# A two-layer decoder trunk: matmul operands moved to multiples of 128 bytes in SBUF, with a padded stride between the K blocks of the activations

## The chip, the cores and the metric

The kernel runs on one core of one Trainium2 chip, as one launch. The metric is the device time of that launch in microseconds (us); a figure for a kernel is the median of several runs. The engines are named as in the profile: PE is TensorE's matrix multiplication, PEld its loading of weights (the stationary operand), DVE is VectorE, ACT is ScalarE, POOL is GpSimd and SP is SyncE, which issues most DMAs.

## What is computed

The reference is a trunk of two decoder layers on one sequence of 256 tokens with 1024 features. Each layer has a feed-forward network (FFN), a token mixer and a second FFN. Ahead of each stands an RMS norm whose output is shifted and scaled by values that come from a conditioning vector `c`; behind each, a gate from `c` scales what is added to the stream.

```python
for layer in range(DEPTH):                       # DEPTH = 2
    if layer == N_A_LAYERS:                      # keys, values and forget gates, once
        k_sh, v_sh, F_sh = shared_kv(x, c_act, ...)
    mod = c_act @ ada_w[layer] + ada_b[layer]    # shifts, scales and gates
    h = modulate(rms_norm(x, norm_g[layer, 0]), sh1, sc1)
    x = x + 0.5 * g1 * swiglu(h, ffn_w_in[layer, 0], ffn_w_out[layer, 0])
    h = modulate(rms_norm(x, norm_g[layer, 1]), sh2, sc2)
    mix = diff_attention(h, ...) if layer < N_A_LAYERS else forgetting_attention(h, ...)
    x = x + g2 * mix
    h = modulate(rms_norm(x, norm_g[layer, 2]), sh3, sc3)
    x = x + 0.5 * g3 * swiglu(h, ffn_w_in[layer, 1], ffn_w_out[layer, 1])
return rms_norm(x, final_g)
```

`swiglu` is `(silu(h @ w_gate) * (h @ w_up)) @ w_out` with 2816 hidden features. All data are float32.

## The kernel before

**Layout.** Features lie on the 128 partitions, tokens along the free axis. The stream `x`, the normed input and the hidden features are therefore arrays of blocks of 128 features by 256 tokens. The normed input, 8 such K blocks, is held as two tiles, `HH` and `HL` (lines 391 and 392); the hidden features as 11 pairs of tiles `hidh0` to `hidh10` and `hidl0` to `hidl10` (lines 526 and 527), each with two K blocks of 256 columns.

**Three products for one.** A float32 number is split into a high part of type float32r and the rest, also float32r. A product then is three matmuls into the same PSUM bank (`mm3`, line 383): high weight by high input, low weight by high input, high weight by low input. `HH`, `hidh` and `wh` are high parts; `HL`, `hidl` and `wl` low ones. Nearly every matmul has a 128x128 weight block as its stationary operand, and 256 columns of the input as the moving one; each has its own weight load, which runs while the matmul ahead of it streams. Where the input is taken ahead of its norm (tiles lp, lg, lu), two extra columns beside each K block of `HH` and `HL` carry the shift: a row of a K block has `SX` = 258 floats. In the V projection (`v_proj`, line 698) the roles are exchanged: blocks of `HH` and `HL` are stationary and 512 columns of weights stream.

**The FFN** (`ffn`, line 518). In the first phase a group of 256 gate and 256 up features is made at a time: two banks, `pg` and `pu`, and for each of the 8 K blocks four weight blocks of 128 columns, three matmuls each, 12 matmuls a K block and 96 a group. There are 38 such groups in the four FFNs (7, 10, 11 and 10); the other features of the first FFN are made in eight banks (`pf`), those of the two "late" FFNs in `lg` and `lu`. In the second phase each of 8 output blocks `po` sums 22 K blocks of hidden features, 66 matmuls; K blocks 2j and 2j+1 come from `hidh{j}` and `hidl{j}`. The hidden tiles are used again by the attention layers under other names.

**The weights** come from DRAM in parts of up to 1024 columns into one of six `raw` tiles, are copied to one of six `wh` tiles by ScalarE, and VectorE writes the rest into one of five `wl` tiles (lines 262 to 294).

**Order.** Each engine keeps the order in which the program issues its instructions. `InOrder` (line 56) wraps each engine and runs a rough clock while the program is written out: before an instruction that would have to wait, it puts background work, which is weight splits on ScalarE and VectorE and modulation columns on VectorE. That clock knows when a tile is ready by its name, and for tiles whose names begin with HH, HL or x_ by the offset too (line 83).

**Modulation.** Every shift, scale and gate is a column tile of 8 floats a partition, `mod_...`, with a derived one `modx_...` for scales and some gates (lines 195 and 204). `ada_block` fills one column with a multiply and sum on VectorE.

**The norm.** `rstd_of` (line 433) makes 1/rms: ScalarE writes a first estimate `r0`, VectorE refines it in three steps and writes the last into a tile `rstd` of its own.

**Where tiles lie.** The tiles of a pool are laid one after the other in the order in which the program first asks for them, each rounded up to 32 bytes a partition. A tile's start therefore depends on the small tiles ahead of it: `eps`, `half`, `one`, the modulation columns, `ls`, `nlam`, `subg`, `fb` and `Fq`.

Of the kernel before, what the change touches and what calls it, by code (L numbers as in the profile page):

```python
# [10 lines left out]
F32 = mybir.dt.float32  # L11
F32R = mybir.dt.float32r
BF16 = mybir.dt.bfloat16
AF = mybir.ActivationFunctionType
ALU = mybir.AluOpType
PSUM = bass.MemoryType.PSUM

P = 128
D = 1024
S = 256  # L20
NC = D // P
HD = 64
AH = 8
BH = 16
# [7 lines left out]
K0 = 4  # L32
SX = S + 2
CP_SLACK = 0.3
SUB_SLACK = 0.2
# [20 lines left out]
class InOrder:  # L56
    """An engine whose instructions keep the order of this program.

    A rough clock of each engine (us) tells when background work fits."""

# [10 lines left out]
    def plainly(self, f):  # L71
        """f() without background work before its instructions."""
        busy, self.busy = self.busy, True
        f()
        self.busy = busy

    def __getattr__(self, name):
        f = getattr(self.engine, name)

        def call(*args, **kw):  # L80
            aps = [v for v in (*args, *kw.values()) if hasattr(v, "tensor")]
            if aps:
                names = [(v.tensor.name, v.offset if v.tensor.name[:2] in ("HH", "HL", "x_") else 0) for v in aps]
                cost = self.fixed + self.rate * math.prod(aps[0].shape[1:])
# [21 lines left out]
def trunk(ctx, tc, a, out):  # L106
# [26 lines left out]

# [1 line left out]
    crow = ap_.tile([P, 2, D], F32, tag="ada", name="crow").rearrange("p a b -> p (a b)")  # L135
# [15 lines left out]
    dve.memset(one, 1.0)  # L151
    cact = cp_.tile([P, D], F32, name="cact")

    def table(func):
        act.preload_act_table(func)

# [1 line left out]
    mods = {}  # L158
# [27 lines left out]
    def ada_block():  # L186
        """One column block of one modulation; a load follows each second one."""
        u, i = divmod(ada_done[0], 2)
# [5 lines left out]
        if m not in mods:  # L194
            mods[m] = [cp_.tile([P, NC], F32, name=f"mod_{m[0]}_{m[1]}"), None]
        mt = mods[m][0]
# [5 lines left out]
        if kind != 0 and m[1] != 5:  # L202
            if mods[m][1] is None:
                mods[m][1] = cp_.tile([P, NC], F32, name=f"modx_{m[0]}_{m[1]}")
            mx = mods[m][1]
            js = (j, j + 1) if m == (0, 1) else ((j - 3, j + 1) if j % 4 == 3 else None)
            if js is not None:
                js = slice(*js)
                if kind == 1:
                    gc = V_KVN if m[0] == "kv" else V_NORM + (m[0] * 3 + m[1] // 3) * NC  # L210
                    dve.scalar_tensor_tensor(
                        mx[:, js], mt[:, js], 1.0, vecs[:, gc + js.start:gc + js.stop],
                        op0=ALU.add, op1=ALU.mult)
                else:
                    dve.tensor_scalar_mul(mx[:, js], mt[:, js], 0.5)
# [7 lines left out]

# [1 line left out]
    stream = []  # L225
# [36 lines left out]
    def w_dma(count=NRAW):  # L262
        """Load the next parts of the stream, as far as the parts in their place are split."""
        while count and len(raws) < min(len(pieces), len(los) + NRAW):
# [8 lines left out]
    def cp_part():  # L273
        """Copy the next part of the stream: its high float32r half."""
        u = len(his)
# [7 lines left out]
    def sub_part():  # L283
        """The low half of the oldest copied part; its place takes the next load."""
        u = len(los)
# [13 lines left out]
    def ahead():  # L299
        """Parts copied beyond the unit in use."""  # L300
        return len(his) - begun[0]

    def take(src, split=False):
        """The next unit of the stream, split; blk(c, w) gives its columns."""
        u = taken[0]
# [20 lines left out]
    def work(cols):  # L326
        """After the products of this many columns of the stream."""
        credit[0] = min(CREDIT, credit[0] + pace[0] * 2 * cols / 2048)
        if mode[0] != "hold":
            bg()  # L330
# [6 lines left out]
    def fill_dve(start):  # L337
        """Background work before an instruction that has to wait until start."""
        while mode[0] != "hold" and dve.t + DVE_FIT < start:
# [11 lines left out]
    def bg():  # L351
        """Background work as far as it fits: splits first, then modulations at their pace."""
        while (len(his) < min(len(pieces), len(raws), done[0] + NHI)
# [35 lines left out]

# [1 line left out]
    HH = cp_.tile([P, NC, SX], F32R, name="HH")  # L391
    HL = cp_.tile([P, NC, SX], F32R, name="HL")
    hx = [(HH[:, k], HL[:, k]) for k in range(NC)]
    hn = [(HH[:, k, :S], HL[:, k, :S]) for k in range(NC)]
# [3 lines left out]
    def shift_cols(nxt):  # L398
        """The shift as an extra pair of columns beside the input."""
        shb = mods[nxt[1]][0].rearrange("p (k o) -> p k o", o=1).to_broadcast([P, NC, 2])  # L400
        act.copy(HH[:, :, S:], shb)
        dve.tensor_tensor(HL[:, :, S:], shb, HH[:, :, S:].bitcast(F32), op=ALU.subtract)

    def x_update(n, ps, gate, nxt, acc_eng):
        """x[n] += gate * ps; then g*(1+scale)*x[n] for the next product, and the square of x[n].

        Returns the second half, for VectorE after ScalarE's part."""
        dve.scalar_tensor_tensor(x[n], ps, gate[:, n:n + 1], x[n], op0=ALU.mult, op1=ALU.add)
# [24 lines left out]
    def rstd_of(then=None, parts=None):  # L433
# [10 lines left out]
        dve.scalar_tensor_tensor(ra, ra, -0.5, r0, op0=ALU.mult, op1=ALU.mult)  # L444
        r = kp.tile([P, S], F32, tag="rstd", name="rstd", bufs=1)
        dve.scalar_tensor_tensor(r, ra, 1.5, r0, op0=ALU.add, op1=ALU.mult)
        return r

    def make_h(k, r, m):
        """h[k]; returns VectorE's second half."""  # L450
        A, sh = mods[m[0]][1], mods[m[1]][0]
# [7 lines left out]
    class MakeH:  # L459
        """h chunk by chunk, VectorE's second half of each behind the first half of the next."""  # L460

# [22 lines left out]
    def late_pairs(src, dsts, m, then):  # L484
        """Two pairs of blocks of W against the input before its norm; the outputs go to dsts, normalised.

        Returns 1/rms."""
        pb = []
# [27 lines left out]

# [1 line left out]
    def ffn(l, i, kind, m, nxt, at=2):  # L518
        """kind: 1/rms for the first FFN; "late" if hx is not normalised; "ready" if it is."""
        hid = []  # L520
# [140 lines left out]
    class OutProj:  # L661
        """Residual product whose K blocks come one at a time, the last two together."""

# [7 lines left out]
        def steps(self):  # L671
            """The next K block, in eight steps."""
            k = self.k
# [24 lines left out]
    def v_proj(src, dst):  # L698
        """dst[t][nh]: [P tokens, 512 features]; a step is one K block of one half."""
        for nh in range(2):  # L700
# [18 lines left out]
    def pair_proj(src, dst, name):  # L719
        """Two 128-feature blocks of h @ W, transposed, in eight steps."""  # L720
        pq = mmbank(name)
# [13 lines left out]

# [1 line left out]
    ada_dma(2)  # L737
# [25 lines left out]

# [1 line left out]
    UW = 383  # L765
    late = {}

    def constants():
# [5 lines left out]
        sp.dma_start(raw[:, o:a["misc"].shape[1]], a["misc"][:, o:])  # L774
        # relative position bias (times 8, with the mask), skewed through DRAM
        hot, umask, relb = raw[:NB, o:o + UW], raw[:AH, o + UW:o + 2 * UW], raw[:NB, o + 2 * UW:o + 2 * UW + AH]
        o += 2 * UW + AH

        def bias():
# [9 lines left out]
            late["skew"] = skew  # L789
            # -lambda on every partition  # L790
            ls = cp_.tile([P, 2], F32, name="ls")
            lj = kp.tile([P, HD], F32, tag="w512a", name="lj")
            for i in range(2):
# [3 lines left out]
            act.activation(ls, ls, AF.Exp)  # L797
            nlam = cp_.tile([P, 1], F32, name="nlam")
            dve.scalar_tensor_tensor(nlam, ls[:, 1:2], -LAMBDA_INIT, ls[:, 0:1],
                                     op0=ALU.add, op1=ALU.subtract)  # L800
            subg = cp_.tile([P, 1], F32, name="subg")
            dve.tensor_scalar_mul(subg, vecs[:, V_SUB:V_SUB + 1], 1.0 - LAMBDA_INIT)
# [4 lines left out]

    # ================= layer A =================
    pace[0] = PACE[0]
# [165 lines left out]

    # ================= shared keys, values and forget gates =================
    kT = [cp_.tile([P, 512], F32, name=f"kT{j}") for j in range(4)]
# [32 lines left out]
    for i, (kk, n) in enumerate(v_proj("wkv", vb)):  # L1010
# [9 lines left out]
        if i == 3:  # L1020
# [3 lines left out]
            mm(pF[:, BH:2 * BH], ub[:, :P], lft[:, BH:], start=False, stop=True)  # L1024
            Fq = cp_.tile([P, 2 * BH], F32, name="Fq")
            act.copy(Fq, pF[:, :2 * BH])
# [13 lines left out]

    # ================= layer B =================
    pace[0] = PACE[4]
# [251 lines left out]
```

## Time and profile before

| | |
|---|---|
| time, median of 3 runs | 1038.09 us (1037.96 to 1039.49) |
| span of the profiled execution (first to last instruction) | 1035.3 us |
| median less that span | 2.8 us |
| mean granted TensorE clock | 0.997 |
| DMA | 265.06 MB, mean 256 GB/s |
| VectorE: weight splits `wl`, 368 instructions | 402.5 us |
| ScalarE: weight casts `wh`, 368 instructions | 349.1 us |
| VectorE: modulation columns, 160 instructions | 203.6 us |

For the profiled execution the span is the only time that is given; the runs' times are those of other executions of the same program. A row of a group in the profile has the line, the engine, the operation, output and inputs by the program's names, shape and count, then busy time and the mean duration of one in ns. Since all engine calls go through one helper, every row shows line 101, and a group is known by its tiles. The duration of a matmul runs from its start to its modelled end, and matmuls overlap; how fast they follow each other is read from their starts in the timeline (start, duration, engine, operation). In the table of stretches a row has the stretch, its length, and for PE, PEld, DVE, ACT and POOL the busy time with the number of instructions, then the granted clock, the DMA engines' busy share and GB/s.

### The profile page before, as it was taken

To read this page: it belongs to the slowest core of one execution; us is meant where nothing else is said; L and a number is where in the kernel's file an instruction comes from. 1 tells how busy PE (TensorE), PEld (TensorE's weight loads), DVE (VectorE), ACT (ScalarE), POOL (GpSimd) and SP (SyncE) were. 2 spreads that over 40 slices of the span, in tenths; PEclk is the share of its full clock that TensorE was granted. 3 is DMA by queue.
4 is the path that set the end of the run, shared out by engine and by line. 5 is a ranking of instruction groups with operands and counts; after the bars stand their busy time and mean duration, and the time that the engine had idled before them with its cause. 6 is when DMAs were issued, how large, how long until landed. Compare 5 with 4: busy or idle time off the path is not lost.

```text
span 1035.3 us, 20394 instructions
## 1 busy us (share of the span) xinstructions
PE 1013.1 (98%) x8076; PEld 975.6 (94%) x8076; DVE 820.8 (79%) x1379; ACT 563.2 (54%) x922; POOL 38.2 (4%) x64
## 2 busy tenths in 40 slices
PE   5999999999999999999999999999999999999996
PEld 4999999998999999999998999999987799999996
DVE  6978869889889998778798888879887697555553
ACT  4465545576777644445566444444575585444542
POOL 0000100000111000000000000000011010000000
PEclk9999999999999999999999999999999999999998
DMA  9988999969666798778867999888744337554561
GB/s 350 413 301 273 308 351 340 337 202 343 196 211 219 250 400 304 271 266 303 301 226 265 345 315 334 317 282 320 263 147 121 116 126 229 185 183 147 164 173 41
DMA packets 68130, 265.06 MB, mean 256 GB/s; under 512 B 7962, under 2 KB 8114, under 8 KB 57923
## 3 DMA queue, kind: packets, MB, share of 16 engines
q1 hardware_dynamic: 65810, 258.31, 71.6%
q0 software_dynamic: 1792, 4.81, 1.7%
q8 instruction: 63, 1.03, 0.4%
q10 hardware_dynamic: 432, 0.64, 0.2%
q14 instruction: 33, 0.26, 0.1%
HBM read 262.66 MB, written 2.65 MB: 256 GB/s over the span
## 4 chain that ended last, share of the span: by engine, by line
PE 93%; ACT 2%; DVE 2%; issue 1%; DMA 1%; POOL 1%; SPq 0%; DVEq 0%; ACTq 0%; POOLq 0%
PE po L101 24%; PE pg L101 21%; PE pu L101 21%; PE pf L101 5%; PE pv L101 4%; PE pw L101 3%; PE lp L101 3%; PE pqk L101 2%; PE pob L101 1%; PE lg L101 1%; PE lu L101 1%; PE pk L101 1%; PE sb L101 1%; ACT nl L101 1%; PE pq L101 1%
## 5 line engine op out<-in xcount | busy, mean ns | idle before, releaser
L101 DVE TENSOR_TENSOR wl<-raw,wh 128x1024 fp32r<-128x1024 f32 (+1 forms) x368 | 402.5, 1106 | 114.7 <-issue 29.9
L101 ACT CAST wh<-raw 128x1024 fp32r<-128x1024 f32 (+1 forms) x368 | 349.1, 956 | 239.7 <-PE pu L101 117.3
L101 DVE CUSTOM_DVE_ANT_0 ada<-ada,cact,vecs 128x1024 f32<-128x1024 f32 x160 | 203.6, 1280 | 0.0
L101 PE MATMUL po<-hidh,wh 128*128 128x256 f32 x704 | 198.0, 281 | 0.0
L101 PE MATMUL po<-hidl,wh 128*128 128x256 f32 x704 | 197.8, 281 | 0.0
L101 PE MATMUL po<-hidh,wl 128*128 128x256 f32 x704 | 197.7, 281 | 0.0
L101 PE MATMUL pg<-HH,wl 128*128 128x256 f32 x608 | 172.0, 283 | 0.0
L101 PE MATMUL pg<-HL,wh 128*128 128x256 f32 x608 | 172.0, 283 | 0.0
L101 PE MATMUL pu<-HL,wh 128*128 128x256 f32 x608 | 171.7, 282 | 0.0
L101 PE MATMUL pu<-HH,wl 128*128 128x256 f32 x608 | 171.5, 282 | 0.0
L101 PE MATMUL pg<-HH,wh 128*128 128x256 f32 x608 | 170.9, 281 | 0.0
L101 PE MATMUL pu<-HH,wh 128*128 128x256 f32 x608 | 170.8, 281 | 0.0
L101 PEld LDWEIGHTS po<-hidh,wh 128*128 128x128 f32 x704 | 132.8, 189 | 0.0
L101 PEld LDWEIGHTS po<-hidh,wl 128*128 128x128 f32 x704 | 132.5, 188 | 0.0
L101 PEld LDWEIGHTS po<-hidl,wh 128*128 128x128 f32 x704 | 132.5, 188 | 0.0
L101 PEld LDWEIGHTS pg<-HH,wh 128*128 128x128 f32 x608 | 115.2, 189 | 0.7 <-issue 0.6
L101 PEld LDWEIGHTS pu<-HH,wh 128*128 128x128 f32 x608 | 115.3, 190 | 0.0
L101 PEld LDWEIGHTS pg<-HL,wh 128*128 128x128 f32 x608 | 115.0, 189 | 0.0
L101 PEld LDWEIGHTS pu<-HL,wh 128*128 128x128 f32 x608 | 114.8, 189 | 0.0
L101 PEld LDWEIGHTS pu<-HH,wl 128*128 128x128 f32 x608 | 114.6, 188 | 0.0
L101 PEld LDWEIGHTS pg<-HH,wl 128*128 128x128 f32 x608 | 114.3, 188 | 0.0
L101 ACT CAST hidh<-hf 128x512 fp32r<-128x512 f32 x44 | 27.3, 621 | 35.6 <-DVE hf L101 35.6
(213 smaller groups left out, 1610.4 us busy)
## 6 DMA issues: line engine op xcount, KB each, us to landing
raw<-in_win SPq DMA_DIRECT2D x176, 512.0 KB, 6.0
ada<-in_ada SPq DMA_DIRECT2D x79, 1024.0 KB, 7.3
raw<-in_wout SPq DMA_DIRECT2D x64, 384.0 KB, 4.9
raw<-in_wout SPq DMA_DIRECT2D x64, 320.0 KB, 4.2
raw<-in_wqk SPq DMA_DIRECT2D x16, 512.0 KB, 5.5
raw<-in_wo SPq DMA_DIRECT2D x16, 512.0 KB, 4.6
raw<-in_wv SPq DMA_DIRECT2D x8, 512.0 KB, 6.0
raw<-in_wkk SPq DMA_DIRECT2D x8, 512.0 KB, 6.6
```

The costliest lines, as they stand in the source:

```text
L101: return self.tc.keep_in_program_order(f(*args, **kw))
```

## The change

`HH` and `HL` get rows of 288 floats in place of 258, so that a K block begins every 1152 bytes, 9 x 128; the two shift columns still stand at 256 and 257. The small tiles that lay between the large ones are collected in `small` (24 floats) and `modall` (33 x 8 floats), whose sizes, with those of the small tiles ahead of them, add up to a multiple of 128 bytes, and `Fq` is widened to 56 floats for the same purpose. `HH`, `HL`, the hidden tiles and what shares their places, `tri`, `kT`, `vb`, `raw`, `wh`, `wl` and the `qk` tiles then begin at multiples of 128 bytes; `ones` doesn't. The tile `rstd` goes: the last refinement is written over `r0`, which makes room for the padding. The planner keeps apart slices of tiles whose names begin with "mo" by their offset. All shapes and numbers that are computed stay as they were. Comments and docstrings are blank lines.

```diff
+SP_ = 288
...
-                names = [(v.tensor.name, v.offset if v.tensor.name[:2] in ("HH", "HL", "x_") else 0) for v in aps]
+                names = [(v.tensor.name, v.offset if v.tensor.name[:2] in ("HH", "HL", "x_", "mo") else 0) for v in aps]
...
     cact = cp_.tile([P, D], F32, name="cact")
+    small = cp_.tile([P, 24], F32, name="small")
+    nmods = [0]
+    modall = cp_.tile([P, 33, NC], F32, name="modall")
+
+    def mod_col():
+        nmods[0] += 1
+        return modall[:, nmods[0] - 1]
...
-            mods[m] = [cp_.tile([P, NC], F32, name=f"mod_{m[0]}_{m[1]}"), None]
+            mods[m] = [mod_col(), None]
...
-                mods[m][1] = cp_.tile([P, NC], F32, name=f"modx_{m[0]}_{m[1]}")
+                mods[m][1] = mod_col()
...
-    HH = cp_.tile([P, NC, SX], F32R, name="HH")
-    HL = cp_.tile([P, NC, SX], F32R, name="HL")
-    hx = [(HH[:, k], HL[:, k]) for k in range(NC)]
+    HH = cp_.tile([P, NC, SP_], F32R, name="HH")
+    HL = cp_.tile([P, NC, SP_], F32R, name="HL")
+    hx = [(HH[:, k, :SX], HL[:, k, :SX]) for k in range(NC)]
...
-        act.copy(HH[:, :, S:], shb)
-        dve.tensor_tensor(HL[:, :, S:], shb, HH[:, :, S:].bitcast(F32), op=ALU.subtract)
+        act.copy(HH[:, :, S:SX], shb)
+        dve.tensor_tensor(HL[:, :, S:SX], shb, HH[:, :, S:SX].bitcast(F32), op=ALU.subtract)
...
-        r = kp.tile([P, S], F32, tag="rstd", name="rstd", bufs=1)
-        dve.scalar_tensor_tensor(r, ra, 1.5, r0, op0=ALU.add, op1=ALU.mult)
-        return r
+        dve.scalar_tensor_tensor(r0, ra, 1.5, r0, op0=ALU.add, op1=ALU.mult)
+        return r0
...
-            ls = cp_.tile([P, 2], F32, name="ls")
+            ls = small[:, :2]
...
-            nlam = cp_.tile([P, 1], F32, name="nlam")
+            nlam = small[:, 2:3]
...
-            subg = cp_.tile([P, 1], F32, name="subg")
+            subg = small[:, 8:9]
...
-            Fq = cp_.tile([P, 2 * BH], F32, name="Fq")
+            Fq = cp_.tile([P, 56], F32, name="Fq")[:, :2 * BH]
```

## The prediction

> **What bounds the kernel now.** I read the page first: span, engines, granted clock, and the chain that ended last.
>
> ```profile
> span 1035.3 us, 20394 instructions
> PE 1013.1 (98%) x8076; PEld 975.6 (94%) x8076; DVE 820.8 (79%) x1379; ACT 563.2 (54%) x922; POOL 38.2 (4%) x64
> ...
> PEclk9999999999999999999999999999999999999998
> ...
> PE 93%; ACT 2%; DVE 2%; issue 1%; DMA 1%; POOL 1%; SPq 0%; DVEq 0%; ACTq 0%; POOLq 0%
> ```
>
> TensorE is busy for 98% of the span at the full clock, and 93% of the last chain is its own work. So the time is the number of matmuls times the distance from one start to the next. That distance is not the "mean ns" of a group, since matmuls overlap in the pipeline; it has to be read from starts. The page gives the counts:
>
> ```profile
> L101 PE MATMUL po<-hidh,wh 128*128 128x256 f32 x704 | 198.0, 281 | 0.0
> L101 PE MATMUL pg<-HH,wl 128*128 128x256 f32 x608 | 172.0, 283 | 0.0
> ```
>
> There are three forms of each (high by high, low by high, high by low): 3 x 704 = 2112 down-projection matmuls (po) and 6 x 608 = 3648 gate and up matmuls (pg, pu). The code adds 1344 of the kind that reads HH or HL: pf 8 x 16 x 3 = 384, lp 288, pqk 288, lg, lu, pk and pq 96 each. So 4992 matmuls stream HH or HL and 2112 stream a hidden tile.
>
> The next view is the stretch table over two gate/up groups of 96 matmuls, then TensorE's timeline of the first of them, cut to the row that begins each K block (12 matmuls each).
>
> ```profile
> 641.86:653.32 11.46, 11.46 (x99) 11.46 (x97) 9.72 (x12) 5.43 (x7) 0.00 (x0) 1.00 0.99 381
> ```
> ```profile
> 871.10:882.56 11.46, 11.46 (x98) 11.46 (x97) 6.10 (x6) 5.48 (x7) 0.00 (x0) 1.00 0.59 196
> ```
> ```profile
> 641.86 0.29 PE L101 MATMUL pg<-HH,wh 128*128 128x256 f32 x1
> ...
> 643.28 0.28 PE L101 MATMUL pg<-HH,wh 128*128 128x256 f32 x1
> ...
> 644.73 0.28 PE L101 MATMUL pg<-HH,wh 128*128 128x256 f32 x1
> ...
> 646.15 0.28 PE L101 MATMUL pg<-HH,wh 128*128 128x256 f32 x1
> ...
> 647.60 0.28 PE L101 MATMUL pg<-HH,wh 128*128 128x256 f32 x1
> ...
> 649.03 0.28 PE L101 MATMUL pg<-HH,wh 128*128 128x256 f32 x1
> ...
> 650.46 0.28 PE L101 MATMUL pg<-HH,wh 128*128 128x256 f32 x1
> ...
> 651.88 0.28 PE L101 MATMUL pg<-HH,wh 128*128 128x256 f32 x1
> ...
> 653.32 0.29 PE L101 MATMUL pg<-HH,wh 128*128 128x256 f32 x1
> ```
>
> Two things are to be seen. First, both groups take 11.46 us, 119.4 ns a matmul, although in one VectorE worked 9.72 us and the DMA engines were 0.99 busy at 381 GB/s, and in the other 6.10 us and 0.59 at 196 GB/s. Whatever sets 119.4 ns is inside TensorE and its own operand reads; what the other engines do to SBUF does not show. That leaves room for addresses to matter. Second, the K blocks are not equal: blocks 0, 2, 4, 6 take 1.42, 1.42, 1.43, 1.42 us, together 5.69 (118.5 ns a matmul); blocks 1, 3, 5, 7 take 1.45, 1.45, 1.43, 1.44, together 5.77 (120.2 ns).
>
> **What the addresses are.** In the program before, each tile starts at the end of the one before it, rounded up to 32 bytes. Added up from the declared sizes, modulo 128, HH starts at 0, HL at 64, each weight tile wh and wl at 96, hidden tiles at 96, but hidden 5 and 6 at 32. A row of HH has 258 floats, 1032 bytes, so K block k of HH starts at 8k and of HL at 64 + 8k: only the even blocks begin at a multiple of 16. After the change all of these are at 0 (row 1152 bytes, 9 x 128). Only `ones`, used by 26 matmuls, stays at 32.
>
> **Edit 1: HH and HL blocks at 0 instead of 8k.** The odd blocks are the only ones off a multiple of 16, and the only ones that are slow. Block 0, which already starts at 0 and 64, takes 1.42 us like blocks 2, 4 and 6, whose starts are only multiples of 16. So I expect the odd blocks to fall to the even ones, and nothing from the further step to 128. A group gains 5.77 - 5.69 = 0.08 us; 4992 / 96 = 52 groups give 52 x 0.08 = 4.2 us, all on the path. Bounds: each row is rounded to 0.01 us, so 0.04 to 0.12 us a group, 2.1 to 6.2 us.
>
> The Trainium skill has this rule: "SBUF — State Buffer", section "Door 1: The DMA port swizzle", says in its box on cachelines that SBUF lines are 16 bytes and that crossing into a new one is paid for. The slow odd blocks agree with it. By that rule alone the change would give the 4.2 us here and nothing anywhere else, as all other operands already start at multiples of 32; that speaks against most of the change.
>
> **Edit 2: weights from 96 to 0.** Here the stationary side has a row of its own. In the V projection HH is stationary and the weights stream, 512 columns at a time, six matmuls a K block:
>
> ```profile
> 550.49 0.40 PE L101 MATMUL pv<-wh,HH 128*128 128x512 f32 x1
> ...
> 551.89 0.40 PE L101 MATMUL pv<-wh,HH 128*128 128x512 f32 x1
> ...
> 560.25 0.40 PE L101 MATMUL pv<-wh,HH 128*128 128x512 f32 x1
> ```
> ```profile
> L101 PEld LDWEIGHTS pg<-HH,wl 128*128 128x128 f32 x608 | 114.3, 188 | 0.0
> ```
> ```profile
> L101 PEld LDWEIGHTS pv<-wh,HH 128*128 128x128 f32 x64 | 12.0, 188 | 3.4 <-issue 0.8
> ```
>
> Block 0, with its stationary operand at 0 and 64, takes 1.40 us; blocks 1 to 6 take 8.36 us, 1.39 each. A weight load takes 188 ns on average both from wl, always at 96, and from HH, at eight different residues. An aligned stationary operand is worth nothing here. I put this edit at 0 by itself; what it does jointly with the moving operand is the open question, and the rivals price it.
>
> **Edit 3: hidden tiles to 0, like the weights.** Now moving and stationary operand have the same residue everywhere. The down projection before has both: hidden 0 to 4 (K blocks 0 to 9) and the weights are all at 96, while hidden 5 and 6 (K blocks 10 to 13) are at 32. Two output blocks in a row, each cut at K blocks 0, 10 and 14:
>
> ```profile
> 464.03 0.28 PE L101 MATMUL po<-hidh,wh 128*128 128x256 f32 x1
> ...
> 467.59 0.28 PE L101 MATMUL po<-hidh,wh 128*128 128x256 f32 x1
> ...
> 468.95 0.28 PE L101 MATMUL po<-hidh,wh 128*128 128x256 f32 x1
> ...
> 471.78 0.28 PE L101 MATMUL po<-hidh,wh 128*128 128x256 f32 x1
> ...
> 475.34 0.28 PE L101 MATMUL po<-hidh,wh 128*128 128x256 f32 x1
> ...
> 476.76 0.28 PE L101 MATMUL po<-hidh,wh 128*128 128x256 f32 x1
> ...
> 479.60 0.29 PE L101 MATMUL po<-hidh,wh 128*128 128x256 f32 x1
> ```
>
> With both at 96, 30 matmuls take 3.56 us in either output block, 118.7 ns. With hidden at 32, 12 matmuls take 1.36 us (113.3 ns) in the first and 1.42 us (118.3 ns) in the second, with the same addresses; so the spacing also has a memory of its own, two ways in which loads and streams can interlock. My reading is that the interlock depends on where the two operands stand to each other, and that equal residues at 0 behave like equal residues at 96: 118.7 ns, which also is what the even HH blocks show. Then hidden 5 and 6 lose their good half: 12 x 118.7 = 1.42 us in place of 1.36, 0.06 us in 16 of the 32 output blocks, +1.0 us, and nearly nothing in the other 16. Bounds: 0 if they keep it, and, if everything takes the good interlock, a large gain (below).
>
> **The rest at nothing.** 1/rms is written back into r0, so ScalarE's next write of r0 must wait for the last reader of 1/rms. The norms are far apart, and the readers are the first chunks of the layer that follows:
>
> ```profile
> L101 DVE SCALAR_TENSOR_TENSOR rstd<-ra,r x7: 424/424/426, 14.8 to 1028.5; 128x256 f32<-128x256 f32 x7
> ```
>
> Seven in 1014 us; were the cover gone, ScalarE's weight casts behind that write would wait, and TensorE lives on up to six cast parts. The modulation columns become slices of one tile, and HH's blocks already are slices of one tile whose writers and readers overlap without cost, so I see no new wait. In the helper's rough clock the sums into these columns are now booked at offset 0, so a few background casts may change places; with ScalarE at 54% I put that at 0, within 1 us either way.
>
> **The sum.** -4.2 + 1.0 = -3.2 us against a span of 1035.3, so 1032.1. The median of the three runs, 1038.1, lies 2.8 us above the span; I carry that over: **1034.9 us**. Its own range, from the bounds of the terms (-6.2 to -1.1, and 1 us of order), is 1031 to 1038.
>
> **The rivals.**
> *All matmuls take the good interlock.* If the excess over 113.3 ns is there because at least one of the two operands is always off 0, then with both at 0 every matmul may go at 113.3. Then 4992 x (119.4 - 113.3) = 30.5 us, and for po, which now takes 7.75 and 7.82 us for 66 matmuls, 118.0 ns, 2112 x 4.7 = 9.9 us: 40 us less, **997.7 us**. For it: the good spacing exists in the trace, for four K blocks in every second output block, and no row has both operands at 0. Against it: either operand alone at 0 gains nothing. DMA (0.99 in the first stretch above) would be late next, but it runs ahead elsewhere. The Trainium skill goes further: "TensorE: Matmul & The Clock Gate", section "Back-to-back issue gap", has a gap of N / 2.4 + 2.5 ns, 109.2 ns for 256 columns, an estimate by which the change could give 4992 x 10.2 + 2112 x 8.8 = 69 us; the trace, at 119.4 ns with the clock at 1.00, disagrees with it so far.
>
> *Slower: equal residues everywhere collide.* If two streams that start at the same residue hit the same part of SBUF in step, the spacing may settle at that of the slowest block shown, 1.45 / 12 = 120.8 ns, in HH and hidden alike: 4992 x 1.4 + 2112 x 2.8 = +12.9 us, **1051 us**. It decides from 119.0 ns, the present mean of both kinds. Against it: both at 96 is such a case, and goes at 118.7.
>
> *The change does nothing here.* The slow odd blocks could come from their place in the sequence and not their address, and the hidden tiles keep their mean: **1038 us**.
>
> **Chances.** The forecast 0.50; the good interlock, whole or in large part, 0.25; nothing 0.12; the collision 0.13. About 0.2%, 2 us, is what a measurement of this kernel can tell from no change. Two thirds of the forecast's cases are faster than 1036.0, the rest within: faster 0.33 + 0.25 = 0.58, same 0.16 + 0.12 = 0.28, slower 0.14 with an unlucky order. The range for 8 in 10 reaches to the good interlock in full, 997, and on the other side to a third of the collision, 1042.
>
> **What would show it.** In the profile after: a gate/up group at 11.38 us with equal K blocks of 1.42 us, the po output blocks all alike at 7.83 us with no 1.36 us stretch. Equal K blocks well under 1.40 us would show the good interlock and refute the argument that one aligned operand would have shown it; blocks of 1.44 us or more the collision; odd blocks still slower than even ones would refute the address as their cause.

## The result, and the profile after

The changed kernel takes 1039.9 us (median of 13 runs, 1038.74 to 1041.62) where the kernel before took 1036.85 (median of 13 runs, 1034.82 to 1039.49, the three of the table above among them): ratio 1.003, 95% interval 1.0021 to 1.0038. It is slower by some 3 us, 0.3%. The two profiled executions differ by 1.7 us, 1037.0 against 1035.3; single runs of one kernel spread by 3 to 5 us, so two executions need not differ as the medians do. From the page after:

```profile
span 1037.0 us, 20397 instructions
PE 1015.5 (98%) x8076; PEld 978.1 (94%) x8076; DVE 822.1 (79%) x1379; ACT 564.0 (54%) x922; POOL 37.9 (4%) x64
...
L102 PE MATMUL po<-hidh,wh 128*128 128x256 f32 x704 | 199.2, 283 | 0.0
...
L102 PEld LDWEIGHTS po<-hidl,wh 128*128 128x128 f32 x704 | 135.1, 192 | 0.0
```

TensorE has the same matmuls and is 2.4 us longer at them; the busy times of the other engines are within 1.3 us of those before. The weight loads of the down projection now last 192 ns on average, in the kernel before 188 to 189. The starts say where the time is. TensorE's timeline of the kernel after, a gate/up group cut at K blocks 0, 1, 2 and at its end, and two down-projection outputs cut at K blocks 0, 10 and 14:

```profile
642.10 0.28 PE L102 MATMUL pg<-HH,wh 128*128 128x256 f32 x1
...
643.52 0.28 PE L102 MATMUL pg<-HH,wh 128*128 128x256 f32 x1
...
644.95 0.28 PE L102 MATMUL pg<-HH,wh 128*128 128x256 f32 x1
...
653.51 0.28 PE L102 MATMUL pg<-HH,wh 128*128 128x256 f32 x1
```
```profile
463.85 0.28 PE L102 MATMUL po<-hidh,wh 128*128 128x256 f32 x1
...
467.45 0.28 PE L102 MATMUL po<-hidh,wh 128*128 128x256 f32 x1
...
468.89 0.28 PE L102 MATMUL po<-hidh,wh 128*128 128x256 f32 x1
...
471.77 0.28 PE L102 MATMUL po<-hidh,wh 128*128 128x256 f32 x1
...
479.69 0.28 PE L102 MATMUL po<-hidh,wh 128*128 128x256 f32 x1
```

A group takes 11.41 us in place of 11.46, with K blocks of 1.42 and 1.43 that are now alike. An output takes 7.92 us in place of 7.75 and 7.82, 120.0 ns a matmul, and the same in every part: 3.60 us for 30 matmuls, 1.44 for 12. So 38 groups give back 0.05 us each, 1.9 us, and 32 outputs cost 0.135 us each against the mean of before, 4.3 us: 2.4 us worse, as much as TensorE's busy time grew. The other 1344 matmuls that read HH or HL take as long as before, 172 us in all from start to start.

### The profile page after: what moved, and what is told of

Same layout as the page of the kernel before. It is cut to its first block, busy times and chain, and to the rows that moved or that the text cites. A ratio compares the mean times of both kernels' runs of the same rounds, so it can differ in the third digit from the quotient of the medians.

```text
span 1037.0 us, 20397 instructions
## 1 busy us (share of the span) xinstructions
PE 1015.5 (98%) x8076; PEld 978.1 (94%) x8076; DVE 822.1 (79%) x1379; ACT 564.0 (54%) x922; POOL 37.9 (4%) x64
## 4 chain that ended last, share of the span: by engine, by line
PE 93%; ACT 2%; DVE 2%; issue 1%; DMA 1%; POOL 1%; SPq 0%; DVEq 0%; ACTq 0%; POOLq 0%
PE po L102 25%; PE pu L102 21%; PE pg L102 21%; PE pf L102 5%; PE pv L102 4%; PE pw L102 4%; PE lp L102 3%; PE pqk L102 2%; PE pob L102 1%; PE lg L102 1%; PE lu L102 1%; PE pk L102 1%; PE sb L102 1%; ACT nl L102 1%; PE pq L102 1%
## 5 line engine op out<-in xcount | busy, mean ns | idle before, releaser
L102 PEld LDWEIGHTS po<-hidl,wh 128*128 128x128 f32 x704 | 135.1, 192 | 0.0
L102 PEld LDWEIGHTS po<-hidh,wl 128*128 128x128 f32 x704 | 135.1, 192 | 0.0
L102 PEld LDWEIGHTS po<-hidh,wh 128*128 128x128 f32 x704 | 135.1, 192 | 0.0
L102 ACT ACTIVATE HH<-ht,modall 128x256 fp32r<-128x256 f32 x56 | 27.8, 507 | 39.1 <-DVE ht L102 36.6
```

The source lines that it names most:

```text
L102: return self.tc.keep_in_program_order(f(*args, **kw))
```

## The experiments

**Three theories.** I count addresses modulo 256 from here on, and call the moving operand's start minus the stationary operand's the distance. In the kernel before, weights started at 224; the distance of HH was 160 + 8k, of HL 224 + 8k, of hidden 0 to 4 and 8 to 10 it was 128, of hidden 5 and 6 it was 192, of hidden 7 it was 0. After the change it is 0 for all hidden tiles and for even K blocks, 128 for odd ones (rows of 1152 bytes, 4.5 x 256). Theory *relative*: this distance sets the spacing. Rival *absolute*: starting at multiples of 128 (or 64) does. Rival *order*: neither; the modulation columns' new names moved some background work, and that costs the time.

**1. Everything 32 bytes further.** HH, HL, the hidden tiles and the weights no longer start at multiples of 128; all distances stay.

```diff
-    small = cp_.tile([P, 24], F32, name="small")
+    small = cp_.tile([P, 32], F32, name="small")
```

> Everything from the modulation tile on moves up by 32 bytes (`small` from 24 to 32 floats): HH, HL, hidden tiles and weights all start at 32 modulo 128, none at a multiple of 128, and they stand to each other exactly as in the changed kernel. Theory 'relative' (the spacing of matmuls is set by where the moving operand starts relative to the stationary one): as the changed kernel, 120.0 ns a matmul in the down projection and 11.41 us for a gate/up group of 96. Rival 'absolute' (starting at a multiple of 128 is itself what makes it 120.0 and evens out the K blocks): other values, towards those of the kernel before, 118.0 ns and 11.46 us. Rival 'order' (the moved background work on ScalarE and VectorE costs the time, not the addresses): 120.0 too, since the order is that of the changed kernel.

Time 1039.51 us in one run, span 1037.6. Its timeline, one group and one output:

```profile
642.69 0.28 PE L102 MATMUL pg<-HH,wh 128*128 128x256 f32 x1
...
654.11 0.28 PE L102 MATMUL pg<-HH,wh 128*128 128x256 f32 x1
```
```profile
464.46 0.28 PE L102 MATMUL po<-hidh,wh 128*128 128x256 f32 x1
...
472.38 0.28 PE L102 MATMUL po<-hidh,wh 128*128 128x256 f32 x1
```

11.42 and 7.92 us: as the changed kernel, although none of these operands starts at a multiple of 128. *Absolute* falls.

**2. and 3. Only the weights moved, by 64 and by 192 bytes.** All starts are still multiples of 64. The edit of w64 is shown; w192 has 104 in place of 72.

```diff
-            Fq = cp_.tile([P, 56], F32, name="Fq")[:, :2 * BH]
+            Fq = cp_.tile([P, 72], F32, name="Fq")[:, :2 * BH]
```

> The changed kernel with `Fq` 64 bytes longer, so that raw, wh and wl start at 64 modulo 256 and all activations stay where they are: the hidden tiles now stand 192 bytes (modulo 256) past the weights, as hidden 5 and 6 did in the kernel before. Theory 'relative': the down projection leaves 120.0 ns and goes to the 113.3 ns that hidden 5 and 6 showed in every second output block, or to their other value of 118.3; gate/up groups change too, even K blocks as the down projection. Rival 'absolute at 64' (only whether an operand starts at a multiple of 64 counts): 120.0 and 11.41 us as in the changed kernel. Rival 'order': 120.0 and 11.41 us.

> The same with 192 bytes: weights at 192 modulo 256, the hidden tiles stand 64 past them. Theory 'relative': a spacing of its own, not 120.0; if only the distance modulo 128 counts it is that of w64, if modulo 256 it differs from w64. The odd K blocks of the gate/up group here have the distance that the even ones have in w64. Rivals 'absolute at 64' and 'order': 120.0 and 11.41 us.

w64 took 1025.52 us, w192 1030.18, each in one run (kernel before, same chip: 1035.77; shift32, same chip: 1039.51). Timelines of an output in the second feed-forward network of each, and of one in the first of w64:

```profile
456.59 0.28 PE L102 MATMUL po<-hidh,wh 128*128 128x256 f32 x1
...
464.37 0.28 PE L102 MATMUL po<-hidh,wh 128*128 128x256 f32 x1
```
```profile
157.55 0.28 PE L102 MATMUL po<-hidh,wh 128*128 128x256 f32 x1
...
165.03 0.28 PE L102 MATMUL po<-hidh,wh 128*128 128x256 f32 x1
```
```profile
460.92 0.28 PE L102 MATMUL po<-hidh,wh 128*128 128x256 f32 x1
...
468.69 0.28 PE L102 MATMUL po<-hidh,wh 128*128 128x256 f32 x1
```

7.78 us (117.9 ns) at distance 192 in the second network, 7.48 us (113.3 ns) at the same distance in the first; 7.77 us at distance 64. With the same instructions in the same order on every engine, moving the weights alone takes away 9 to 14 us against shift32. *Order* falls as the cause, and *absolute at 64* with it. Distance 192 has two spacings, as hidden 5 and 6 had; distance 64 showed the wider one only, in all four networks of its one trace. That the distance modulo 128 is not enough is surer from the distances 0 and 128: 120.0 ns in the down projection here, and 118.7 ns with hidden 0 to 4 in the kernel before.

**4. Eight distances in one group.**

```diff
-SP_ = 288
+SP_ = 264
```

> The changed kernel with rows of HH and HL of 264 floats, 1056 bytes: K block k of both starts 32k past a multiple of 256, so that the eight K blocks of a gate/up group have the eight distances 0, 32, ..., 224 to the weights; hidden tiles and weights stay at 0. Theory 'relative': the K blocks differ, each with the spacing of its distance (block 0 near 120 ns, block 4, at 128, near 118.6, block 6, at 192, between 113.3 and 118.3), and the down projection stays at 120.0. Rival 'absolute': only block 4 and block 0 start at multiples of 128 and are alike, the others are alike among themselves or go by multiples of 64. Rival 'order': all K blocks at 1.43 us as in the changed kernel.

1036.43 us in one run. The timeline of a group at K blocks 0, 5, 7 and its end:

```profile
640.40 0.28 PE L102 MATMUL pg<-HH,wh 128*128 128x256 f32 x1
...
647.52 0.28 PE L102 MATMUL pg<-HH,wh 128*128 128x256 f32 x1
...
650.34 0.28 PE L102 MATMUL pg<-HH,wh 128*128 128x256 f32 x1
...
651.76 0.28 PE L102 MATMUL pg<-HH,wh 128*128 128x256 f32 x1
```

Blocks 5 and 6 (distances 160 and 192) take 2.82 us, 117.5 ns a matmul; blocks 0 to 4 take 7.12 us, 118.7. Over a whole network, blocks 0 to 7 take 118.9, 118.3, 118.2, 118.8, 118.5, 117.4, 117.7 and 118.3 ns a matmul. The blocks differ, but by little, and block 0 is not near the 120 ns that I expected: a distance held for 12 matmuls only doesn't reach what it comes to when it is held throughout. The groups of the changed kernel show the same, 118.8 ns at distance 0 and 119.0 at 128.

**5. and 6. The two parts of the change apart.** One is the kernel before with the padded rows alone:

```diff
+SP_ = 288
...
-    HH = cp_.tile([P, NC, SX], F32R, name="HH")
+    HH = cp_.tile([P, NC, SP_], F32R, name="HH")
...
-        dve.scalar_tensor_tensor(r, ra, 1.5, r0, op0=ALU.add, op1=ALU.mult)
+        dve.scalar_tensor_tensor(r0, ra, 1.5, r0, op0=ALU.add, op1=ALU.mult)
```

The other is the changed kernel with rows of 258 floats, HH, HL, hidden tiles and weights shifted so that HH and HL have the distances of the kernel before:

```diff
-SP_ = 288
+SP_ = 258
...
-    small = cp_.tile([P, 24], F32, name="small")
+    small = cp_.tile([P, 64], F32, name="small")
...
-    HL = cp_.tile([P, NC, SP_], F32R, name="HL")
+    HL = cp_.tile([P, NC * SP_ + 56], F32R, name="HL")[:, :NC * SP_].rearrange("p (k s) -> p k s", k=NC)
```

> The kernel before with one part of the change: rows of 288 floats in HH and HL (and 1/rms written over r0, which makes the room). All K blocks of HH and HL start at multiples of 128 bytes relative to each other and none has 8 bytes over a multiple of 16; hidden tiles and weights stay at 96 and 32 modulo 128 and stand to each other as before. My reading in the prediction: odd K blocks fall to the even ones, 11.38 us a gate/up group. Theory 'relative' (the distance from the weights' start to the moving operand's, modulo 256, sets the spacing): the distances are now 32 in even and 160 in odd blocks, which took 118.2 and 117.4 ns in map32, so 11.31 us a group, 8 us less in all; the down projection keeps 118.0 ns. Rival 'absolute': the blocks are off 128-byte alignment to the weights, and nothing is gained over 11.41 us.

> The other part alone: hidden tiles and weights start at multiples of 256 as in the changed kernel, while HH and HL have their rows of 258 floats back and stand to the weights as in the kernel before. Theory 'relative': the down projection at 120.0 ns as in the changed kernel, gate/up groups at 11.46 us as before; so slower than the changed kernel by about 2 us, and by 4 us than the kernel before. Rival 'order': the down projection's 120.0 ns came with other parts of the change; no forecast that the two kinds separate so.

The padded rows alone took 1032.23 us, the hidden tiles alone 1040.88, each in one run (kernel before, same chip: 1037.73). The two don't add up to the change, since the padded rows stand at distances 32 and 160 here and at 0 and 128 there. Padded rows alone, a group at K blocks 0, 1, 2 and its end, and two outputs; then one output and one group of the other kernel:

```profile
638.42 0.28 PE L102 MATMUL pg<-HH,wh 128*128 128x256 f32 x1
...
639.82 0.28 PE L102 MATMUL pg<-HH,wh 128*128 128x256 f32 x1
...
641.26 0.28 PE L102 MATMUL pg<-HH,wh 128*128 128x256 f32 x1
...
649.78 0.28 PE L102 MATMUL pg<-HH,wh 128*128 128x256 f32 x1
```
```profile
461.20 0.28 PE L102 MATMUL po<-hidh,wh 128*128 128x256 f32 x1
...
468.96 0.28 PE L102 MATMUL po<-hidh,wh 128*128 128x256 f32 x1
...
476.78 0.29 PE L102 MATMUL po<-hidh,wh 128*128 128x256 f32 x1
```
```profile
464.68 0.28 PE L102 MATMUL po<-hidh,wh 128*128 128x256 f32 x1
...
472.60 0.28 PE L102 MATMUL po<-hidh,wh 128*128 128x256 f32 x1
```
```profile
643.33 0.29 PE L102 MATMUL pg<-HH,wh 128*128 128x256 f32 x1
...
654.79 0.29 PE L102 MATMUL pg<-HH,wh 128*128 128x256 f32 x1
```

The parts separate: padded rows leave the outputs at 7.76 and 7.82 us; hidden tiles at distance 0 give 7.92, in a kernel whose groups take 11.46 us as before. That kernel has the instructions of the changed one in their order, other starts than the kernel before, but its distances in HH and HL, and each of its K blocks takes what it took there to within 0.1 ns a matmul. *Relative* missed the padded group: 11.36 us against 11.31 forecast, and the blocks the other way about, 1.40 (distance 32) and 1.44 (160). A short block's time depends on its neighbours too. But all these blocks start at multiples of 128 from each other, and odd and even still differ, so 8 bytes over a multiple of 16 are not needed for that; whether they had a share in it before is not shown.

**7. and 8. Distance 192 everywhere.** First w64 again, timed; then (d192) with rows of 1280 bytes, 5 x 256, so that odd K blocks have distance 192 too. Three temporary tiles take the places of others to make the room.

```diff
-SP_ = 288
+SP_ = 320
-        ra = kp.tile([P, S], F32, tag="ra", name="ra", bufs=1)
+        ra = kp.tile([P, S], F32, tag="lt", name="ra")
...
-    fg = kp.tile([P, NC, BH], F32, tag="fg", name="fg", bufs=1)
+    fg = kp.tile([P, NC, BH], F32, tag="acc", name="fg")
...
-            Fq = cp_.tile([P, 56], F32, name="Fq")[:, :2 * BH]
+            Fq = cp_.tile([P, 72], F32, name="Fq")[:, :2 * BH]
...
-            lft = kp.tile([P, 2 * BH], F32, tag="lft", name="lft", bufs=1)
+            lft = kp.tile([P, 2 * BH], F32, tag="acc", name="lft")
```

> The kernel of w64 again, timed. From its one look 1.0% faster than the kernel before; theory 'relative' holds that this is a property of the layout: ratio 0.988 to 0.992. It had two ways of interlocking at the same distance of 192 (113.3 ns in the first feed-forward network after an interruption of TensorE, 117.8 in the others); if the way is a matter of chance, times of single runs should spread by several us.

> As w64, with rows of 320 floats in HH and HL, 1280 bytes, so that every K block, even and odd, starts 192 bytes past the weights modulo 256 (two small tiles share other places to make the room). Theory 'relative': even and odd K blocks are alike, either at 117.8 ns (11.31 us a group, time as w64) or, where the good interlock holds, at about 113.4 (10.9 us a group); in the first feed-forward network after the interruption both kinds at 113.4. If all of the feed-forward networks took the good one, 1038 - 38 = 1000 us. Rival 'only hidden tiles can take it': gate/up groups stay at 11.31 us everywhere.

w64: 1024.6 us, ratio 0.9878 (0.9862 to 0.9895), single runs within 0.5 us. d192: 1015.21 us, ratio 0.9789 (0.9774 to 0.9803). The timeline of d192, a group in the second network and one in the third:

```profile
380.54 0.28 PE L102 MATMUL pg<-HH,wh 128*128 128x256 f32 x1
...
391.84 0.28 PE L102 MATMUL pg<-HH,wh 128*128 128x256 f32 x1
```
```profile
626.10 0.28 PE L102 MATMUL pg<-HH,wh 128*128 128x256 f32 x1
...
636.98 0.28 PE L102 MATMUL pg<-HH,wh 128*128 128x256 f32 x1
```

11.30 us, and 10.88 us or 113.3 ns a matmul. The first and third networks ran at 113.3 ns, the second and fourth, which begin with the 258-column matmuls, at 117.8. The rival that only hidden tiles can take the narrow spacing falls.

**9. and 10. An interruption after the 258-column matmuls**, in d192 and, as a control, in the changed kernel:

```diff
             j0 = 1
+            mm(abank("kick")[:, :P], ones, ones, start=True, stop=True)
         for j in range(j0, NG):
```

> d192 with one float32 matmul of 128 columns on `ones` (its result is not read) between the 258-column phase and the first gate/up group of the two late feed-forward networks, which are the two that stay at 117.8 ns. Theory 'phase' (at distance 192 there are two ways of interlocking; which one holds is set where the stream was last interrupted, and the 258-column matmuls leave it in the slow one): the interruption lets it settle again, both late networks go to 10.88 us a group and 113.3 ns in the down projection, 2 x (10 x 0.43 + 8 x 0.29) = 13 us less than d192, near 1002 us. Rival 'chance': the late networks stay at 11.31 us, or one of them changes; about 1015 us.

> The changed kernel with the same two extra matmuls, as a control: at distance 0 only one spacing of the down projection has been seen, 120.0 ns, before and after interruptions. Theory 'phase': no change but the cost of the two matmuls, below 1 us; 120.0 ns stays. Rival: if the interruption alone brings the good interlock, whatever the distance, the two late networks fall below 120.0 ns.

d192_kick: 1006.05 us (1002.31 to 1008.03), ratio 0.9686 (0.9662 to 0.971). The control: 1039.59 us in one run, as the changed kernel. A group in d192_kick's second network and one in its first:

```profile
384.25 0.28 PE L102 MATMUL pg<-HH,wh 128*128 128x256 f32 x1
...
395.13 0.28 PE L102 MATMUL pg<-HH,wh 128*128 128x256 f32 x1
```
```profile
84.52 0.28 PE L102 MATMUL pg<-HH,wh 128*128 128x256 f32 x1
...
95.83 0.28 PE L102 MATMUL pg<-HH,wh 128*128 128x256 f32 x1
```

Both late networks went to 10.88 us a group. The first network, which the edit doesn't touch, had 11.31 in this execution, where d192 had 10.88. One program can do both: the third group of w64's first network, in its first and in its second profiled execution:

```profile
85.62 0.28 PE L102 MATMUL pg<-HH,wh 128*128 128x256 f32 x1
...
96.93 0.28 PE L102 MATMUL pg<-HH,wh 128*128 128x256 f32 x1
```
```profile
84.80 0.28 PE L102 MATMUL pg<-HH,wh 128*128 128x256 f32 x1
...
95.92 0.28 PE L102 MATMUL pg<-HH,wh 128*128 128x256 f32 x1
```

11.31 and 11.12 us: in the first network it is decided anew from execution to execution. Seven groups and eight outputs between the two spacings are 7 x 0.43 + 8 x 0.29 = 5.3 us, about the spread of the single times; that the spread is this was not traced. The control shows that an interruption alone does nothing at distance 0. Nor is it enough at distance 192: in the fifth group of the first network a float32 matmul (pb) stands between the others in every kernel. Behind it w64's first execution went from 11.31 to 11.12 us a group, but d192_kick stayed at 11.31.

**11. and 12. How wide the place is.** d192_kick with `Fq` of 64 and of 80 floats, distances 224 and 160.

> d192_kick with the weights 32 bytes lower: moving operands 224 past the weights in every matmul. Theory 'relative' gives no number for a distance that has not been held over a whole group; in map32 the block at 224 took 118.4 ns between neighbours at other distances. It tells how wide the good place is: 113.3 ns here would make it at least 32 bytes wide on this side. Rival 'multiples of 64': 224 behaves as 192 or as 256.

> d192_kick with the weights 32 bytes higher: moving operands 160 past the weights. In map32 the block at 160 took 117.4 ns, the least of the eight. Theory 'relative': a spacing of its own for all groups alike, between 113.3 and 118.6; 113.3 would make the good place at least 32 bytes wide on this side.

1033.49 and 1032.58 us, each in one run. One output of each in the second network, 224 first, and one of 160 in the first network:

```profile
461.39 0.28 PE L102 MATMUL po<-hidh,wh 128*128 128x256 f32 x1
...
469.20 0.28 PE L102 MATMUL po<-hidh,wh 128*128 128x256 f32 x1
```
```profile
461.77 0.28 PE L102 MATMUL po<-hidh,wh 128*128 128x256 f32 x1
...
469.51 0.28 PE L102 MATMUL po<-hidh,wh 128*128 128x256 f32 x1
```
```profile
160.56 0.28 PE L102 MATMUL po<-hidh,wh 128*128 128x256 f32 x1
...
168.39 0.28 PE L102 MATMUL po<-hidh,wh 128*128 128x256 f32 x1
```

7.81 us (118.3 ns) at 224; 7.74 us (117.3 ns) and 7.83 us (118.6 ns) at 160, which has two spacings as well: the outputs have the smaller in the second and fourth network, the larger in the first and third. The 113.3 ns of distance 192 was not seen 32 bytes to either side. Distances 32, 64, 96 and 128 were not tried in all matmuls with the interruption.

## Why the prediction was wrong

- **What bounds the kernel** held: the time moved with the spacing of matmuls, and with nothing else of this size that the runs show.
- **Edit 3 is the step that failed**: "equal residues at 0 behave like equal residues at 96: 118.7 ns". I had reduced the addresses modulo 128. Hidden 0 to 4 and the weights were both at 96 modulo 128, but at 96 and 224 modulo 256, 128 bytes apart. The rows that I read as "equal" were not a case of it; distance 0 proper, held throughout, is 120.0 ns. The term came to +4.3 us where I had +1.0, since hidden 0 to 4 and 8 to 10 lost too, and not only 5 and 6. Experiment 6 shows the loss by itself: outputs of 7.92 us with groups as before.
- **Edit 1** had its direction: the K blocks became alike. Its size was 1.9 us in place of 4.2. A group gained 0.05 us in place of 0.08, because the blocks met at 118.8 and 119.0 ns and not at the 118.5 that I had read for the even ones, and the matmuls outside the 38 groups, 14 groups' worth in my sum, gained nothing. Its reason is not borne out: experiments 4 to 6 show distances to the weights at work, and blocks that all start at multiples of 32 still differ, by up to 3 ns in experiment 5. The box of the Trainium skill on 16-byte lines ("SBUF — State Buffer", "Door 1: The DMA port swizzle"), which I had taken as agreeing, does not explain that difference.
- **Edit 2** at 0 "by itself" was an argument about one operand at a time. It held for what it said: the V projection, where HH is stationary, takes 44.8 us after and 45.1 before, from start to start. But it was empty: moving the weights alone by 64 bytes (w64 against shift32) is worth 1.3%, since it changes every distance.
- **The rest at nothing** held: the reused r0 and the moved background work show no cost; hid_only has both, and its groups take 11.46 us as in the kernel before.
- **The rivals.** The collision came nearest, in the down projection alone, at 120.0 ns in place of the 120.8 that I priced; that the two operands hit the same part of SBUF was not seen. The good interlock exists and is worth most of what I gave it (1006 us with distance 192 against 997.7), but not with both operands at 0, where I had put it. I gave these two 0.13 and 0.25. The formula N / 2.4 + 2.5 ns that I set beside the good interlock is in its section of the Trainium skill ("TensorE: Matmul & The Clock Gate", "Back-to-back issue gap") that of an isolated matmul, not of a stream with weight loads. No spacing that held in any run here was below 113.3 ns.
- **What the two misses add up to.** From the -3.2 us of the sum to the +2.4 that TensorE's time grew are 5.6 us: 3.3 of Edit 3 and 2.3 of Edit 1. With Edit 1 at its forecast size Edit 3 alone would have brought the sum to about nothing. The 1034.9 us also stood on a median of three runs, 1038.1; in 13 runs the kernel before took 1036.85.

## What to carry to other kernels

Where each matmul has its own weight load, read the starts and not the durations, and compare stretches that differ in nothing but addresses. What counted here was where the moving operand starts relative to the stationary one, modulo 256 bytes, and not the alignment of either to 128; modulo 128 was too little, and a bigger modulus was not needed in d192, where neighbouring K blocks differ by 256 modulo 512 and go alike. The layout to look for is one with the same good distance for every K block, which makes the row stride a multiple of 256 too. Before a residue is called equal, the modulus has to be tested.

## What the hardware showed that I had not expected

- Two spacings are the same from one matmul to the next: 113.3 ns (7.48 us / 66) and 120.0 ns (7.92 / 66). The other values, 117.8 and 118.7, are means: there the starts lie 117 to 119 and 115 to 122 ns apart, in patterns that repeat every few matmuls. The weight loads of the down projection went from 188 to 192 ns. Which read waits for which was not measured, nor why 192 is the good distance.
- At distance 192 two spacings, 113.3 and 117.8 ns, each hold for hundreds of matmuls, and so do 117.3 and 118.6 at distance 160; where they changed within a network (w64, d160_kick), the float32 matmul pb stood between. What decides between them stays open: one float32 matmul ahead of the late networks brought the narrow one in both; pb, inside the first network, brought it in one execution of w64 and not in that of d192_kick.
- Another kernel with the same distances at other addresses repeats the time of a K block to 0.1 ns a matmul (hid_only and the kernel before, shift32 and the changed kernel). Where a distance has two spacings, even the same program need not.
